# Context scan of a gated DeltaNet: second direction's values and inverses in the other half of the partitions, products in turn with the first's

## The chip, the cores and the metric

The kernel runs on one core of a Trainium2 chip. The core has a matrix engine (TensorE, PE in the profile, with its weight loads as PEld), a vector engine (VectorE, DVE), a scalar engine (ScalarE, ACT), a general one (GpSimd, POOL), and a queue (SyncE, SP) from which most DMA transfers are issued. Each engine takes its instructions in order and waits on semaphores for the others. The metric is the device time of one execution in microseconds (us).

## The reference

One layer of a diffusion backbone over 512 latent tokens and 256 context tokens, model width 1024, everything in float32: a modulated RMS norm, one wide input projection, two mixers side by side (windowed attention; a gated DeltaNet in both directions), a gated sum, an output projection, and a squared-ReLU MLP. Only the latent tokens' result is returned. The part that the change touches is the DeltaNet, with 8 heads of 64 and chunks of 64 tokens:

```python
def gated_delta_chunked(q, k, v, g_log, beta, s0):
    ...
    t_mat = jnp.eye(CHUNK, dtype=jnp.float32) + bc[..., :, None] * dec_strict * kk
    eG = jnp.exp(G)
    w_mat = lax.linalg.triangular_solve(t_mat, (bc * eG)[..., None] * kc, ...)
    u_v = lax.linalg.triangular_solve(t_mat, bc[..., None] * vc, ...)
    intra = dec_incl * jnp.einsum('bhnid,bhnjd->bhnij', qc, kc)
    ...
    def step(S, xs):
        w_c, uv_c, qd_c, intra_c, kt_c, gl_c = xs
        u = uv_c - jnp.einsum('bhck,bhkv->bhcv', w_c, S)
        o = jnp.einsum('bhck,bhkv->bhcv', qd_c, S) + jnp.einsum('bhij,bhjv->bhiv', intra_c, u)
        S = jnp.exp(gl_c)[..., None, None] * S + jnp.einsum('bhck,bhcv->bhkv', kt_c, u)
        return S, o

def bidir_delta(q, k, v, g, beta, s0_f, s0_b):
    o_f, s_f = gated_delta_chunked(q, k, v, g[:, :, 0], beta[:, :, 0], s0_f)
    flip = lambda a: jnp.flip(a, axis=1)
    o_b, s_b = gated_delta_chunked(flip(q), flip(k), flip(v), flip(g[:, :, 1]), flip(beta[:, :, 1]), s0_b)
    return o_f + flip(o_b), s_f, s_b
```

The context (4 chunks) is scanned from a zero state, in both directions, and only its final states are used. The latent tokens (8 chunks) are scanned from those states, and their outputs of the two directions are added.

## The kernel before

Tensors lie with channels on the 128 partitions and tokens along the free axis. Large projections are computed with each operand split in a high and a low part and three matmuls (`mm3`, lines 317 to 319; the gate tiles' L1028 and L1073 are the same three). Weights come 512 KB at a time over the SP queue into four buffers (`wr`); ACT writes the high part (L259) and DVE the low part (L266). The modulation of the later half of the layer is 32 further loads of 512 KB into the same four buffers and a DVE sum for each (`late_mod`, L1092 and L1094), the "late sums".

The instructions are written in one program order, and a planner then orders each engine's queue ahead of time: whatever it reckons to be ready, with the earlier in program order first. `weave` and the numbers in `FILL` set how pieces of work alternate in program order. The *filler* is a generator that yields after every single matmul: 96 of the attention branch's projection (`br_a`, L1073) and 336 of gate tiles (L1028), 432 in all; `run_fill(n)` takes n of them, `run_both(n)` also issues one late sum for every 12, `run_late(n)` issues late sums alone.

The DeltaNet stage runs in these steps. The triangular inverses are computed on DVE (`invert`, L856 and L857) in 32-row halves, then joined by `combine` (L877 to L901: 32x32 products, copies by ACT, zeros by POOL) into `XA[0]` for the context and `XA[1]` for the latent chunks, one tensor for each direction. `to_tokens` (L910, L915) turns keys and values of four chunks to token-major tensors `KTM` and `VTM`: two heads at a time on the two halves of the partitions, a head pair q in columns q*64.

`chain_step(d, step)` is one step of the scan in direction d, a generator in three parts; `steps` runs the two directions' parts one behind the other. Part 1 multiplies the state with the keys (z, L1152; for latent chunks with the queries too) and makes R on DVE (L1156, L1157). Part 2 multiplies R with the inverse (u, L1164) and scales it (L1170). Part 3 multiplies u with the keys (L1185), for latent chunks also with the score matrices `IA` (L1189), and makes the new state (L1199 on ACT, L1201 on DVE). In the second half of the latent scan the two directions' outputs of a chunk are added there and squared and summed (L1211 to L1215). Each product is 64x64 by 64x64, one head in one corner of the array: rows are the half where its operands lie, columns the half where its result goes. In float32 each is two records of the profile.

```python
    weave((steps(range(NCC)), 3 * NCC), (inv, 40), (fill, FILL[0]), (rest(), 9))
```

This line is the context scan: 12 parts of steps, 40 pieces of the latent chunks' inverses, 144 fillers and 9 pieces of `rest` (L657 to L669 and L910). After it come the latent inverses' transposes (L867) and `combine` twice, each with 36 fillers; the score matrices (`half_products`, L777; L1278 to L1289) in two groups g, each with 36 fillers by `run_both`; and the latent scan with 8, 7 and 3 fillers behind the parts and a late sum in each step. Then the normalised output is transposed (L1323) and split (L185), the last three gate tiles run, and the DeltaNet branch's projection begins (`mm3`, weights `wbr[1]`).

Of the kernel before, what the change touches and what calls it, by code (L numbers as in the profile page):

```python
# [12 lines left out]
ALU = mybir.AluOpType  # L13
# [2 lines left out]

NU = 167
NWR, NWS = 4, 2
FILL = 144, 36, 36, (8, 7, 3)
INV = 2, 12, 18, 0  # L20
QTS = 7, 5, 4, 7, 3, 6, 10, 7
CO = 1
# [77 lines left out]
def tile_layer(ctx: ExitStack, tc: tile.TileContext, I: dict, out: bass.AP, dbg=None):  # L100
# [615 lines left out]
    def col(c):  # L716

        return SEQ + c * CH if c < NCC else (c - NCC) * CH
# [150 lines left out]
    def combine(nto, XTf, XRf, XTb, XRb, XAf, XAb, inplace, between=lambda: None):  # L869

        Y, Ys = bank(), alloc(512)
        nt = v3(nto.ap)
        for i in range(16):
            o = slice(i * HC, (i + 1) * HC)
            for a in range(2):
                lo, hi = quad(a, 0), quad(a, 1)
                PE.matmul(Y[hi, o], nt[lo, i], XRf[lo, i], start=True, stop=True)  # L877
                PE.matmul(Y[lo, o], nt[hi, i], XRb[hi, i], start=True, stop=True)
        A.activation(Ys.ap, Y.ap, AF.Copy)
        Y.free()  # L880
        between()
        XO = bank()
        for i in range(16):
            o = slice(i * HC, (i + 1) * HC)
            for a in range(2):
                lo, hi = quad(a, 0), quad(a, 1)
                PE.matmul(XO[lo, o], Ys[hi, o], XTf[hi, i], start=True, stop=True)
                PE.matmul(XO[hi, o], Ys[lo, o], XTb[lo, i], start=True, stop=True)
        Ys.free()
        xo = v3(XO.ap)  # L890
        if not inplace:
            A.activation(XAf[:, :, :HC], XTf, AF.Copy)
            A.activation(XAb[:, :, :HC], XTb, AF.Copy)
        for a in range(2):
            lo, hi = quad(a, 0), quad(a, 1)
            A.activation(XAf[hi, :, HC:], XTf[hi], AF.Copy)
            A.activation(XAb[hi, :, HC:], XTb[hi], AF.Copy)
            A.activation(XAf[lo, :, HC:], xo[lo], AF.Copy)
            A.activation(XAb[hi, :, :HC], xo[hi], AF.Copy)
# [188 lines left out]
    def late_mod(grp):  # L1088

        for j in range(8):  # L1090
            wa = sb.tile([P, KT, P], F32, tag="wr", bufs=NWR, name=nm("wa")).rearrange("p k c -> p (k c)")
            nc.sync.dma_start(out=wa, in_=I["wada2"][grp, j])  # L1092
            t = alloc(1024)
            V.scalar_tensor_tensor(t.ap, wa, 0.5, scr.ap, op0=ALU.mult, op1=ALU.mult, accum_out=modT[:, grp, j:j + 1])  # L1094
# [43 lines left out]
    def chain_step(d, step):  # L1138
# [4 lines left out]
        m4 = slice(c * 4, c * 4 + 4)  # L1143
        z = zb[d]
        r2 = [slice(0, 64), slice(64, 128)]
        vt = VTM[c // 4][:, c % 4 * 256:(c % 4 + 1) * 256]

        if S is not None:
            for q in range(4):
                for x, src in enumerate((kT, qT) if lat else (kT,)):  # L1150
                    for i, r in enumerate(r2):
                        PE.matmul(z[r2[i ^ x], x * 512 + q * HD:x * 512 + (q + 1) * HD], src[q][r, col(c):col(c) + CH],  # L1152
                                  S[r, q * HD:(q + 1) * HD], start=True, stop=True)
# [3 lines left out]
            V.scalar_tensor_tensor(R, vt, -0.5, R, op0=ALU.mult, op1=ALU.add)  # L1157
        else:
            R = vt
        yield  # L1160
        u = z[:, 256:512]
        for q in range(4):
            for r in r2:
                PE.matmul(u[r, q * HD:(q + 1) * HD], XA[lat][d][r, (cl * 4 + q) * CH:(cl * 4 + q + 1) * CH],  # L1164
                          R[r, q * HD:(q + 1) * HD], start=True, stop=True)
        if S is not None:
            Rb.free()
        if not last:
            uk = alloc(256)
            V.tensor_tensor(hv(uk.ap), hv(u), bc(tb[:, d, m4], HD), op=ALU.mult)  # L1170
        if lat:
            us, zqb = alloc(256), alloc(256)
            zq = zqb.ap
# [30 lines left out]
        if lat:  # L1204
            us.free()
            dst = ot_[:, cl * 256:(cl + 1) * 256]
            if step - NCC < NCL // 2:
                V.tensor_tensor(dst, zq, oi[:, :256], op=ALU.add)
                oi.free()
            else:  # L1210
                V.tensor_tensor(zq, zq, oi[:, :256], op=ALU.add)  # L1211
                oi.free()
                V.tensor_tensor(dst, dst, zq, op=ALU.add)
                A.activation(zq, dst, AF.Square)
                V.tensor_reduce(oss[:, cl], hv(zq), axis=AX.X, op=ALU.add)  # L1215
            zqb.free()

    def steps(r):
# [25 lines left out]
    for b in KTM[:1] + VTM[:1] + XA[0]:  # L1244
        b.free()
    scr = alloc(1024, True)
    nc.sync.dma_start(out=scr.ap, in_=I["crow"][0])
# [10 lines left out]
    for g in range(2):  # L1258
        ms = slice(16 * g, 16 * g + 16)
        f, b = xa[0][:, ms], xa[1][:, ms]  # L1260
        run_fill(FILL[1] - CPAUSE)
        combine(NTO[1 + g], f[:, :, :HC], xr3[0][:, ms], b[:, :, :HC], xr3[1][:, ms], f, b, True, lambda: run_fill(CPAUSE))
        NTO[1 + g].free()
    for b in xr:
        b.free()

    IA = [alloc(2048, True), alloc(2048, True)]
    ia = [v64(b.ap) for b in IA]
    for g in range(2):
        ms = slice(16 * g, 16 * g + 16)  # L1270
        es = slice(512 * g, 512 * g + 512)
        run_both(FILL[2] - FPAUSE)
        qq_ = bank(2)
        qD, qO = diag_off(qq_)
        for _ in half_products(qq_, 1 + g, qT):
# [13 lines left out]
            G.memset(ia[1][lo, ms, HC:], 0.0)  # L1289
    for b in ED + [EO]:  # L1290
        b.free()
    dump("kT0", kT[0].ap)
    dump("qT0", qT[0].ap)

    ot_ = alloc(2048, True)
    ot = ot_.ap.rearrange("p (c q v) -> p c q v", c=NCL, q=4)
# [144 lines left out]
    for hf in range(4):  # L1441
        act_ = []
        for f in range(FT):
# [143 lines left out]
```

## Time and profile before

| | |
|---|---|
| time, median of 3 runs | 912.12 us (910.76 to 913.91) |
| the profiled execution | 911.22 us, its span 909.5 us |
| granted TensorE clock | 1.000 |
| instructions | 16844 |
| chain that ended last, by engine | PE 80%, DVE 10%, ACT 5%, issue 2%, DMA 1% |
| HBM read, written | 102.41 MB, 2.10 MB |

A row of a timeline gives start, duration, engine, line, operation, the buffers written and read (numbers left out; `m` is the arena, `banks` PSUM), the shape, how many instructions, and in brackets how long the engine sat idle before it and whose result it waited for. A row of groups or issues gives a count and a mean or median. In a table by stage each engine's busy time stands with its count of instructions in the order PE, PEld, DVE, ACT, POOL, then the granted clock, the DMA engines' share and GB/s. Matmuls overlap, so the duration of one is longer than the distance to the next; a chain of waits gives the time that each piece added.

### The profile page before, as it was taken

What the parts mean: (1) busy time and instruction counts of PE and PEld (TensorE: products, weight loads), DVE (VectorE), ACT (ScalarE), POOL (GpSimd) and SP (SyncE); (2) the same over time, 40 slices, a digit from 0 to 9 for tenths busy, and PEclk for the clock granted to TensorE, in tenths of its full rate; (3) what the DMA queues carried; (4) which work ended last, traced back from release to release, by engine and by line L of the source; (5) the groups of instructions that cost most, each with busy time, mean ns of one, the idle gap of its engine ahead of it and who ended that gap; (6) DMA issues with size and microseconds to landing.
All of it is one profiled execution on the core that took longest, in us unless ns stands there. A gap on an engine that the chain in (4) does not pass through costs nothing.

```text
span 909.5 us, 16844 instructions
## 1 busy us (share of the span) xinstructions
PE 879.4 (97%) x7082; PEld 704.7 (77%) x7082; DVE 585.4 (64%) x999; ACT 454.9 (50%) x819; POOL 25.2 (3%) x40
## 2 busy tenths in 40 slices
PE   8999999999899999999999999999999999999998
PEld 5668777867677787777678789888888888888886
DVE  3578799887778997677867988941654335324511
ACT  6588755476568786465663445630452134113400
POOL 0010001010000002010000000000000000000000
PEclk9999999999999999999999999999999999999999
DMA  8671455533001133633316773640553224322111
GB/s 355 262 230 21 92 117 120 112 71 58 13 13 35 56 110 94 207 98 95 117 37 219 245 245 135 227 144 1 188 157 95 70 73 150 103 69 79 38 47 46
DMA packets 30460, 105.59 MB, mean 116 GB/s; under 512 B 3760, under 2 KB 4400, under 8 KB 29360
## 3 DMA queue, kind: packets, MB, share of 16 engines
q1 hardware_dynamic: 28368, 97.18, 33.1%
q0 software_dynamic: 2016, 7.34, 5.0%
q8 instruction: 55, 0.90, 0.4%
q14 instruction: 21, 0.17, 0.1%
HBM read 102.41 MB, written 2.10 MB: 115 GB/s over the span
## 4 chain that ended last, share of the span: by engine, by line
PE 80%; DVE 10%; ACT 5%; issue 2%; DMA 1%; SPq 0%; DVEq 0%; ACTq 0%
PE banks L319 16%; PE banks L317 16%; PE banks L318 16%; PE banks L1028 9%; PE banks L424 5%; PE banks L1073 2%; PE banks L429 2%; PE banks L586 2%; PE banks L596 1%; PE banks L1164 1%; ACT m L148 1%; PE banks L662 1%; PE banks L1185 1%; PE banks L1152 1%; PE banks L210 1%
## 5 line engine op out<-in xcount | busy, mean ns | idle before, releaser
L317 PE MATMUL banks<-m,m 128*128 128x512 f32 (+1 forms) x600 | 223.6, 377 | 2.6 <-DVE m L643 1.6
L318 PE MATMUL banks<-m,m 128*128 128x512 f32 (+1 forms) x600 | 224.5, 376 | 0.1
L319 PE MATMUL banks<-m,m 128*128 128x512 f32 (+1 forms) x600 | 224.2, 376 | 0.0
L259 ACT ACTIVATE m<-wr 128x1024 fp32r<-128x1024 f32 x68 | 71.8, 1059 | 155.1 <-PE banks L318 74.0
L317 PEld LDWEIGHTS banks<-m,m 128*128 128x128 f32 x600 | 111.8, 188 | 26.0 <-ACT m L323 2.8
L318 PEld LDWEIGHTS banks<-m,m 128*128 128x128 f32 x600 | 112.5, 188 | 21.9 <-DVE m L324 1.5
L319 PEld LDWEIGHTS banks<-m,m 128*128 128x128 f32 x600 | 112.4, 188 | 21.3 <-issue 1.2
L266 DVE TENSOR_TENSOR m<-wr,m 128x1024 fp32r<-128x1024 f32 x68 | 82.8, 1224 | 62.8 <-ACT m L259 31.2
L1028 PE MATMUL banks<-m,wh 128*128 128x512 f32 x320 | 104.5, 405 | 1.5 <-issue 0.8
L1471 DVE SCALAR_TENSOR_TENSOR m<-banks,modT,m 128x512 f32<-128x512 f32 x32 | 24.0, 750 | 105.3 <-PE banks L319 105.3
L259 ACT ACTIVATE wh<-wr 128x1024 fp32r<-128x1024 f32 (+1 forms) x58 | 54.6, 941 | 50.6 <-issue 11.4
L424 PE MATMUL banks<-m,wh 128*128 128x512 f32 (+1 forms) x320 | 75.9, 374 | 1.2 <-DVE m L823 1.2
L1028 PEld LDWEIGHTS banks<-m,wh 128*128 128x128 f32 x320 | 58.0, 188 | 14.2 <-issue 1.0
L1028 PE MATMUL banks<-m,wl 128*128 128x512 f32 x160 | 64.7, 405 | 0.0
L424 PEld LDWEIGHTS banks<-m,wh 128*128 128x128 f32 x320 | 53.0, 189 | 11.5 <-issue 1.9
L266 DVE TENSOR_TENSOR wl<-wr,wh 128x1024 fp32r<-128x1024 f32 (+1 forms) x44 | 45.2, 1028 | 16.6 <-ACT wh L259 16.5
L184 ACT ACTIVATE m<-m 128x512 fp32r<-128x512 f32 (+1 forms) x56 | 34.8, 629 | 38.1 <-DVE m L1454 21.5
L185 DVE TENSOR_TENSOR m<-m,m 128x512 fp32r<-128x512 f32 (+1 forms) x56 | 38.3, 689 | 21.6 <-ACT m L184 21.3
L1094 DVE SCALAR_TENSOR_TENSOR m<-wa,m 128x1024 f32<-128x1024 f32 x32 | 39.0, 1223 | 12.6 <-DMA wa<-in_wada 7.4
L317 PE MATMUL banks<-m,wh 128*128 128x512 f32 (+1 forms) x120 | 42.0, 352 | 0.0
L319 PE MATMUL banks<-m,wl 128*128 128x512 f32 (+1 forms) x120 | 42.0, 351 | 0.0
L318 PE MATMUL banks<-m,wh 128*128 128x512 f32 (+1 forms) x120 | 41.8, 349 | 0.0
(241 smaller groups left out, 1371.8 us busy)
## 6 DMA issues: line engine op xcount, KB each, us to landing
wr<-in_wm SPq DMA_DIRECT2D x64, 512.0 KB, 3.7
wr<-in_win SPq DMA_DIRECT2D x38, 512.0 KB, 3.7
wa<-in_wada SPq DMA_DIRECT2D x32, 512.0 KB, 4.1
m<-in_wada SPq DMA_DIRECT2D x8, 1024.0 KB, 12.3
wl<-in_win POOLq DMA_DIRECT2D x14, 512.0 KB, 5.7
m<-in_xT SPq DMA_DIRECT2D x8, 512.0 KB, 5.6
wr<-in_wbr SPq DMA_DIRECT2D x16, 256.0 KB, 2.6
wr<-in_wout SPq DMA_DIRECT2D x8, 512.0 KB, 4.6
```

The lines of the kernel that those rows point to most:

```text
L184: A.activation(r32(hi), src, AF.Copy)
L185: (eng or V).tensor_tensor(r32(lo), src, hi, op=ALU.subtract)
L259: h = A.activation(r32(hi), raw, AF.Copy)
L266: V.tensor_tensor(r32(lo), raw, hi, op=ALU.subtract)
L317: PE.matmul(acc, w[0][:, k, :], xhi, start=(start and i == 0), stop=False)
L318: PE.matmul(acc, w[0][:, k, :], xlo, start=False, stop=False)
L319: PE.matmul(acc, w[1][:, k, :], xhi, start=False, stop=(stop and i == n - 1))
L424: PE.matmul(a, w[0][:, k, :], x, start=(k == 0 and x is xs[k][0]), stop=False)
L429: PE.matmul(a, w[1][:, k, :], xs[k][0], start=False, stop=(k == KT - 1))
L1028: PE.matmul(acc.ap, w[x][:, k, :], hx[k][y], start=(k == p == 0), stop=(k == KT - 1 and p == 2))
L1094: V.scalar_tensor_tensor(t.ap, wa, 0.5, scr.ap, op0=ALU.mult, op1=ALU.mult, accum_out=modT[:, grp, j:j + 1])
L1471: V.scalar_tensor_tensor(xn_[ct], acc.ap, modT[:, 3, ct:ct + 1], xn_[ct], op0=ALU.mult, op1=ALU.add)
```

## The change

Context scan. Direction 1's inverses are written to the other half of the partitions (`combine`, not in place). Its values are copied to the other half as `vts` by two DMAs on ACT's queue. Direction 1's z then lands in the half where it didn't before, its R lies there, and u comes back to the natural half. Parts 1 and 2 of a context step yield after each head pair, and `steps` calls the directions in turn, so that the program order of the products is direction 0, direction 1, direction 0, and so on. Part 3 is unchanged.

Latent scan. Twelve fillers are taken before the context scan's weave, which has 132 left. The first part of the first latent step is issued between the score matrices' fillers of the second group. A step has 7, 6, 5 fillers. Added outputs are finished one step later, after part 2 (`add_up`).

Late sums. They write over their own load instead of a fresh buffer, and an order without a wait (`behind`) puts each behind the last chain operation that was issued on DVE. `run_both` stands in `combine`'s stage too (6 more there), the latent scan has 4 instead of 8, and the rest are spread anew.

```diff
-FILL = 144, 36, 36, (8, 7, 3)
+FILL = 132, 36, 36, (7, 6, 5)
 ...
         if not inplace:
             A.activation(XAf[:, :, :HC], XTf, AF.Copy)
-            A.activation(XAb[:, :, :HC], XTb, AF.Copy)
         for a in range(2):
             lo, hi = quad(a, 0), quad(a, 1)
+            blo, bhi = (lo, hi) if inplace else (quad(1 - a, 0), quad(1 - a, 1))
             A.activation(XAf[hi, :, HC:], XTf[hi], AF.Copy)
-            A.activation(XAb[hi, :, HC:], XTb[hi], AF.Copy)
+            if not inplace:
+                A.activation(XAb[blo, :, :HC], XTb[lo], AF.Copy)
+            A.activation(XAb[bhi, :, HC:], XTb[hi], AF.Copy)
             A.activation(XAf[lo, :, HC:], xo[lo], AF.Copy)
-            A.activation(XAb[hi, :, :HC], xo[hi], AF.Copy)
+            A.activation(XAb[bhi, :, :HC], xo[hi], AF.Copy)
             G.memset(XAf[hi, :, :HC], 0.0)
-            G.memset(XAb[lo, :, HC:], 0.0)
+            G.memset(XAb[blo, :, HC:], 0.0)
 ...
-            t = alloc(1024)
-            V.scalar_tensor_tensor(t.ap, wa, 0.5, scr.ap, op0=ALU.mult, op1=ALU.mult, accum_out=modT[:, grp, j:j + 1])
-            t.free()
+            op = V.scalar_tensor_tensor(wa, wa, 0.5, scr.ap, op0=ALU.mult, op1=ALU.mult, accum_out=modT[:, grp, j:j + 1])
+            behind(op)
 ...
-        vt = VTM[c // 4][:, c % 4 * 256:(c % 4 + 1) * 256]
-        if S is not None:
-            for q in range(4):
+        sw = 0 if lat else d
+        vt = (vts if sw else VTM[c // 4])[:, c % 4 * 256:(c % 4 + 1) * 256]
+        for q in range(4):
+            if S is not None:
                 for x, src in enumerate((kT, qT) if lat else (kT,)):
                     for i, r in enumerate(r2):
-                        PE.matmul(z[r2[i ^ x], ...
+                        PE.matmul(z[r2[i ^ x ^ sw], ...
+            if not lat:
+                yield
+        if S is not None:
             Rb = alloc(256)
             R = Rb.ap
-            V.tensor_tensor(hv(R), hv(z[:, 0:256]), bc(eG[:, d, m4], HD), op=ALU.mult)
-            V.scalar_tensor_tensor(R, vt, -0.5, R, op0=ALU.mult, op1=ALU.add)
+            V.tensor_tensor(hv(R), hv(z[:, 0:256]), bc((eGs if sw else eG)[:, d, m4], HD), op=ALU.mult)
+            mark[0] = V.scalar_tensor_tensor(R, vt, -0.5, R, op0=ALU.mult, op1=ALU.add)
 ...
         for q in range(4):
-            for r in r2:
-                PE.matmul(u[r, ...], XA[lat][d][r, ...], R[r, ...], start=True, stop=True)
+            for i, r in enumerate(r2):
+                rr = r2[i ^ sw]
+                PE.matmul(u[r, ...], XA[lat][d][rr, ...], R[rr, ...], start=True, stop=True)
+            if not lat:
+                yield
 ...
-                V.tensor_tensor(dst, dst, zq, op=ALU.add)
-                A.activation(zq, dst, AF.Square)
-                V.tensor_reduce(oss[:, cl], hv(zq), axis=AX.X, op=ALU.add)
+                after.append((dst, zqb, cl))
+                return
 ...
+    def behind(op):
+        if mark[0]:
+            tc.add_manual_dep(op.ins, mark[0].ins.name, nosync, reason="behind the chain")
+
+    def add_up():
+        while after:
+            dst, b, cl = after.pop(0)
+            behind(V.tensor_tensor(dst, dst, b.ap, op=ALU.add))
+            A.activation(b.ap, dst, AF.Square)
+            V.tensor_reduce(oss[:, cl], hv(b.ap), axis=AX.X, op=ALU.add)
+            b.free()
 
     def steps(r):
         for step in r:
             both = [chain_step(d, step) for d in range(2)]
-            for _ in range(3):
-                for g in both:
-                    next(g, None)
+            for n, parts in enumerate((1, 1, 1) if step >= NCC else (5, 5, 1)):
+                for _ in range(parts):
+                    for g in both:
+                        next(g, None)
+                if n == 1:
+                    add_up()
                 yield
+        add_up()
 ...
     to_tokens(VTM, vT, 0)
+    vts = alloc(1024, True)
+    for a in range(2):
+        A.dma_start(out=vts[64 * a:64 * a + 64], in_=VTM[0][64 * (1 - a):64 * (1 - a) + 64])
     to_tokens(KTM, kT, 0)
+    run_fill(12)
 ...
-        run_fill(FILL[1] - CPAUSE)
-        combine(NTO[1 + g], ..., True, lambda: run_fill(CPAUSE))
+        run_both(FILL[1] - CPAUSE)
+        combine(NTO[1 + g], ..., True, lambda: run_both(CPAUSE))
 ...
+    scan = steps(range(NCC, NC_))
     for g in range(2):
-        run_both(FILL[2] - FPAUSE)
+        if g:
+            run_both(FPAUSE)
+            next(scan)
+        run_both(FILL[2] - (1 + g) * FPAUSE)
 ...
-    for n, _ in enumerate(steps(range(NCC, NC_))):
+    for n, _ in enumerate(scan, 1):
         run_fill(FILL[3][n % 3])
-        if n % 3 == 2:
+        if n % 3 == 1 and n < 3 * NCL // 2:
             run_late(1)
 ...
     for _ in gate_tiles(gates[12 + NGD:]):
         pass
+    run_late(2)
 ...
-        run_late(ct % 2)
+        run_late(ct in (2, 5))
 ...
-            if hf == 0:
-                next(late)
+            if hf == 0 and f >= NHALF:
+                for _ in range(1 + (f > NHALF + 1)):
+                    next(late)
```

More of the change, by code (lines that the diff above doesn't have):

```diff
@@ L1162, in chain_step @@
         for q in range(4):
-            for r in r2:
-                PE.matmul(u[r, q * HD:(q + 1) * HD], XA[lat][d][r, (cl * 4 + q) * CH:(cl * 4 + q + 1) * CH],
-                          R[r, q * HD:(q + 1) * HD], start=True, stop=True)
+            for i, r in enumerate(r2):
+                rr = r2[i ^ sw]
+                PE.matmul(u[r, q * HD:(q + 1) * HD], XA[lat][d][rr, (cl * 4 + q) * CH:(cl * 4 + q + 1) * CH],
+                          R[rr, q * HD:(q + 1) * HD], start=True, stop=True)
+            if not lat:
+                yield
         if S is not None:
@@ L1169, in chain_step @@
             uk = alloc(256)
-            V.tensor_tensor(hv(uk.ap), hv(u), bc(tb[:, d, m4], HD), op=ALU.mult)
+            mark[0] = V.tensor_tensor(hv(uk.ap), hv(u), bc(tb[:, d, m4], HD), op=ALU.mult)
         if lat:
@@ L1212, in chain_step @@
                 oi.free()
-                V.tensor_tensor(dst, dst, zq, op=ALU.add)
-                A.activation(zq, dst, AF.Square)
-                V.tensor_reduce(oss[:, cl], hv(zq), axis=AX.X, op=ALU.add)
+                after.append((dst, zqb, cl))
+                return
             zqb.free()
+    after, mark = [], [None]
+    def behind(op):
[8 more added lines that the diff above has]
+            b.free()
     def steps(r):
@@ L1243, in tile_layer @@
         pass
-    for b in KTM[:1] + VTM[:1] + XA[0]:
+    for b in KTM[:1] + VTM[:1] + [vts] + XA[0]:
         b.free()
@@ L1260, in tile_layer @@
         f, b = xa[0][:, ms], xa[1][:, ms]
-        run_fill(FILL[1] - CPAUSE)
-        combine(NTO[1 + g], f[:, :, :HC], xr3[0][:, ms], b[:, :, :HC], xr3[1][:, ms], f, b, True, lambda: run_fill(CPAUSE))
+        run_both(FILL[1] - CPAUSE)
+        combine(NTO[1 + g], f[:, :, :HC], xr3[0][:, ms], b[:, :, :HC], xr3[1][:, ms], f, b, True, lambda: run_both(CPAUSE))
         NTO[1 + g].free()
```

5 lines of the change are left out of this document (2 added, 3 removed).

## The prediction

> **What bounds the kernel now.** I read the page's busy shares first, then a table by stage, then the TensorE timeline of the two scans.
>
> ```profile
> PE 879.4 (97%) x7082; PEld 704.7 (77%) x7082; DVE 585.4 (64%) x999; ACT 454.9 (50%) x819; POOL 25.2 (3%) x40
> ```
> TensorE (PE) is busy nearly always. The table by stage (columns: stretch, length, then busy time of each engine) says where it is not:
> ```profile
> 190.00:290.00 100.00, 93.38 (x760) 71.55 (x759) 75.13 (x131) 69.05 (x124) 3.81 (x6) 1.00 0.13 30
> 290.00:346.80 56.80, 55.38 (x545) 42.28 (x543) 52.96 (x108) 47.98 (x110) 0.34 (x1) 1.00 0.27 80
> 346.80:394.30 47.50, 46.83 (x925) 37.10 (x924) 30.04 (x39) 24.74 (x42) 7.39 (x14) 1.00 0.48 149
> 394.30:474.70 80.40, 74.80 (x1442) 57.96 (x1433) 59.22 (x130) 50.25 (x159) 1.48 (x2) 1.00 0.30 89
> 474.70:560.00 85.30, 84.95 (x452) 72.02 (x451) 70.28 (x116) 36.65 (x58) 0.00 (x0) 1.00 0.66 213
> ```
> 290 to 346.8 is the context scan, to 394.3 the combining of the latent inverses, to 474.7 the latent scan. PE idles 1.4, 0.7 and 5.6 us there, 0.35 us after. So two things count: PE work taken out, and those 7.7 us.
>
> The chain of waits shows what PE work a scan product is (start, us, what):
> ```profile
> 308.91 1.08 PE banks L1152 x32
> 309.98 2.98 PE banks L1073 x12
> 312.97 1.08 PE banks L1164 x32
> 413.41 1.09 PE banks L1152 x64
> ```
> In the context scan a set of products of both directions is 32 records (16 products, two records each) in 1.08 us, 33.7 ns apiece, between 12 filler matmuls; its places in the array alternate between two corners. In the latent scan the same line sends 64 records in 1.09 us, 17.0 ns apiece: there keys and queries go to different corners and all four are used in turn. That row is the price of the change's main idea, measured on the same tile shape.
>
> **The change, part by part.**
>
> *Products in turn.* Direction 1 now multiplies in the two unused corners, and its products alternate with direction 0's, for z (L1152, steps 1 to 3) and u (L1164, steps 0 to 3). Seven sets of 32 records; L1185 stays as it is. A set in full rotation costs 32 x 17.0 ns = 0.545 us and saves 0.535. But TensorE takes its queue in order and the planner puts ready work first, so a set only alternates if both directions' operands are there when it is reached. For z they come early. For u the last operand is direction 1's R (L1157):
> ```profile
> 312.40 0.42 DVE L1157 SCALAR_TENSOR_TENSOR m<-m,m 128x256 f32<-128x256 f32 x1
> 326.08 0.42 DVE L1157 SCALAR_TENSOR_TENSOR m<-m,m 128x256 f32<-128x256 f32 x1
> 339.82 0.42 DVE L1157 SCALAR_TENSOR_TENSOR m<-m,m 128x256 f32<-128x256 f32 x1
> ```
> It ends at 312.82, 326.50, 340.24, and PE takes the sets up at 312.97 and, in the rows below, 327.75 and 341.67: 0.15, 1.25 and 1.43 us to spare. The new filler share (132 over 12 parts: 11 matmuls, not 12) takes one matmul, 2.98/12 = 0.25 us, off each. So z: 3 x 0.535 = 1.6 us. u: two steps of three, 1.07; step 0 none, since its halves already ran apart (next fence). Term: **-2.7 us**, between 0 (nothing alternates) and 7 x 0.535 = -3.75.
> ```profile
> 327.75 1.08 PE banks L1164 x32
> 341.67 1.08 PE banks L1164 x32
> ```
>
> [...]
>
> *Twelve fillers ahead of the scan.* PE timeline:
> ```profile
> 291.91 1.30 PE L910 MATMUL banks<-c_ident,m 128*128 128x128 f32 x8 [0.20 <-DVE m L649]
> 294.10 1.04 PE L1164 MATMUL banks<-m,m 64*64 64x64 f32 x16 [0.89 <-ACT m L915]
> 299.47 0.68 PE L1164 MATMUL banks<-m,m 64*64 64x64 f32 x16
> 303.92 1.15 PE L1185 MATMUL banks<-m,m 64*64 64x64 f32 x32
> ```
> PE waits 0.89 us for the first copies to tokens. Twelve fillers (2.98 us) cover that: **-0.9** (0 to -1.09, the two waits).
>
> *The swapped values (vts).* Two ACT-issued copies, 64 partitions each, between SBUF halves; no such copy is in the trace. Nearest rows:
> ```profile
> wr<-in_win SPq DMA_DIRECT2D x38, 512.0 KB, 3.7
> wr<-in_wbr SPq DMA_DIRECT2D x16, 256.0 KB, 2.6
> 293.57 6.31 ACT L915 ACTIVATE m<-banks 64x256 f32<-64x256 f32 x16
> 345.99 0.33 SPq L250 DMA_DIRECT2D wr<-in_win  x1
> 361.48 0.59 ACT L899 ACTIVATE m<-banks 32x512 f32<-32x512 f32 x1
> ```
> Half of the L915 copies are done at 296.7; two issues (0.33 each) and 2.6 to 3.7 us make 300.0 to 301.1, against 299.47 when direction 1's first products ran. If the planner puts too little filler there, PE waits up to 1.6 us; it can also be nothing. I take **+0.3**, near the lower end, since fillers are ready there. Behind the issues on ACT stand the key copies; they end at 299.9, would end 0.7 later, and L1185 took them at 303.9: covered. The swapped XA costs one more ACT copy of 32 partitions (0.59, as L899) in the attention stage, 190 to 290, where ACT is busy 69.05 of 100 and PE 93.38: mostly covered, **+0.2** for issues and copy (0 to 0.66 + 0.59 = +1.25).
>
> *Latent scan.* PE's waits there:
> ```profile
> 379.47 0.73 PE L1028 MATMUL banks<-m,wh 128*128 128x512 f32 x2 [0.67 <-ACT m L148]
> 400.48 1.15 PE L1164 MATMUL banks<-m,m 64*64 64x64 f32 x32 [1.74 <-DVE m L1157]
> 405.31 0.69 PE L1152 MATMUL banks<-m,m 64*64 64x64 f32 x32 [0.40 <-DVE m L1201]
> 435.87 0.68 PE L1164 MATMUL banks<-m,m 64*64 64x64 f32 x16 [1.09 <-DVE m L1157]
> 444.25 1.15 PE L1164 MATMUL banks<-m,m 64*64 64x64 f32 x32 [0.74 <-DVE m L1157]
> 462.85 0.68 PE L1164 MATMUL banks<-m,m 64*64 64x64 f32 x16 [0.35 <-DVE m L1157]
> ```
> and what VectorE (DVE), and ACT ahead of the first of them, did meanwhile:
> ```profile
> 375.82 2.03 ACT L1199 ACTIVATE m<-m,egl 128x64 f32<-128x64 f32 x8 [1.33 <-DVE m L1094]
> 397.39 1.83 DVE L1285 COPY m<-m 32x512 f32<-32x512 f32 x4
> 403.70 1.22 DVE L1094 SCALAR_TENSOR_TENSOR m<-wa,m 128x1024 f32<-128x1024 f32 x1
> 441.31 0.41 DVE L1213 TENSOR_TENSOR m<-m,m 128x256 f32<-128x256 f32 x1
> 441.64 1.22 DVE L1094 SCALAR_TENSOR_TENSOR m<-wa,m 128x1024 f32<-128x1024 f32 x1
> 461.23 1.22 DVE L1094 SCALAR_TENSOR_TENSOR m<-wa,m 128x1024 f32<-128x1024 f32 x1
> ```
> - The 1.74: the first R stands on DVE behind the scores' copies (L1285). Issued 24 fillers earlier it is out of the way, but u's scaling (L1170) and the output products now stand behind those copies: **-1.2** (0 to -1.74).
> - 0.40 + 0.74 + 0.35 = 1.49: a late sum (L1094, 1.22 us) or a last sum (L1213 and the reduction after it) ahead of a chain step. The change orders them behind: **-1.2** (0 to -1.49).
> - 0.67: ACT held by a buffer that L1094 wrote; in place there is none: **-0.4** (0 to -0.67).
> - The 1.09 has another cause (DVE held by a gate tile and a weight split); 0.
> - New: 7, 6, 5 fillers in place of 8, 7, 3. One filler is 0.25 us less cover after z and after u, eight steps each, where the 0.35 to 1.74 us waits above show little slack: **+0.8** (0 to 16 x 0.25 = +4; the two extra after the third part, 0.5 a step, give half back, so +2).
>
> *Late sums elsewhere.* Twelve of them now fall between 346.8 and 394.3, where DVE idles 17.5 us, in place of six; fewer later. After 474.7 PE idles 0.35 us of 85.3, so nothing is to be won there; the filler and weights hide them. 0, between -0.35 and one sum, +1.22.
>
> *Does the end follow?* The branch after the scan needs the last split:
> ```profile
> 479.90 0.69 DVE L185 TENSOR_TENSOR m<-m,m 128x512 fp32r<-128x512 f32 x1
> 474.71 11.38 PE banks L1028 x49
> ```
> It is ready at 480.6, PE is in gate tiles until 486.1. PE can gain 5.5 us before it would wait, even if DVE's chain (52.96 of 56.80 us busy in the context stage) got no shorter. With 7 fillers left over for the tail, the cover holds.
>
> Sum: -2.7 - 0.9 + 0.3 + 0.2 - 1.2 - 1.2 - 0.4 + 0.8 = **-5.1 us**. The profiled execution took 911.22 us (span 909.5 and 1.7 around it): 906.1. The median of the runs, 912.12, lies 0.9 above it: **907.0**.
>
> **Rivals.**
> 1. *Nothing alternates.* If R of direction 1 comes after PE has begun direction 0's, PE runs 16 and 16 as at 294.10 and 299.47. Sum -2.4: **909.7**. For it: 0.15 us of slack in step 1. Against: over 1 us in the others, more for z.
> 2. *The waits come back elsewhere.* PE's order is fixed when the program is planned; the chip's times differ, and the latent terms (-2.8) turn up at other places. Sum -2.3: **909.8**. For it: six waits of different cause in 85 us.
> 3. *Slower: late loads hold VectorE.* A late sum whose 512 KB have not landed stops DVE, and the next gate weights' low half (L266) behind it:
> ```profile
> 363.30 1.23 DVE L1094 SCALAR_TENSOR_TENSOR m<-wa,m 128x1024 f32<-128x1024 f32 x1 [3.75 <-DMA wa<-in_wada]
> 379.04 1.23 DVE L1094 SCALAR_TENSOR_TENSOR m<-wa,m 128x1024 f32<-128x1024 f32 x1 [3.25 <-DMA wa<-in_wada]
> ```
> Six more of them wait up to 6 x 3.75 = 22.5 us; DVE's 17.5 idle less their own 6 x 1.22 = 7.3 leaves 10.2 of cover. It decides from 10.2 + 5.1 = 15.3 us of waiting. At 18.9, midway to 22.5, the kernel is 3.6 us slower: **915.7**. Against: PE did not stop for L266 at these two; its 0.67 near the second was on ACT.
> 4. *A floor on starts* for alternating products, somewhere between the measured 17.0 and 33.7 ns apiece: at the middle, 25.4, a set saves 0.27, five save 1.35, and the sum is -3.75: **908.4**. [...] The 64-record row speaks against it.
>
> **Chances and range.** Forecast 0.62, rival 1 0.12, rival 2 0.11, rival 3 0.11, rival 4 0.02, else 0.02. A measurement of this kernel tells 0.3% (2.7 us) from no change, so faster is below 909.4: forecast, rival 4 and a third of rivals 1 and 2, 0.72; same 0.16; slower 0.12. The likeliest's own range: all gains in full, -3.75 - 1.09 - 1.74 - 1.49 - 0.67 = -8.7, is 903.4, up to 909.4. The range reaches from 903.0 to 912.0, over rivals 1 and 2; rival 3 is left out.
>
> **What would show it.** Right: L1152 and L1164 in the context scan as mixed sets of 32 records in about 0.55 us; L1185 still 1.08; no 0.89 us wait at the scan's start; in the latent scan no wait of L1164 on L1157 with L1094 ahead of it; PE idle between 290 and 475 about 5 us, not 7.7; br_dn's first matmul 5 us earlier and the tail unchanged. Wrong: sets still 1.08, a wait of L1164 for the vts copy over 1.6 us, or PE waiting on L266 behind an L1094 that waits for its load.

## The result: slightly slower, 915.16 us, and the profile after

The changed kernel took 915.16 us (median of 11 runs, 914.04 to 917.99), the kernel before beside it 912.88 (11 runs, 910.76 to 916.13). The ratio is 1.0028, 95% interval 1.0017 to 1.0039. I had forecast 907.0 with a range of 903.0 to 912.0: wrong in sign, and out by 8.2 us. The profiled execution took 914.04 us (span 912.3), 2.8 more than the one before.

The busy shares hardly differ from before:

```profile
PE 880.7 (97%) x7082; PEld 705.7 (77%) x7082; DVE 587.4 (64%) x999; ACT 455.3 (50%) x820; POOL 25.1 (3%) x40
```

The table by stage does (columns: stretch, length, busy time of PE, PEld, DVE, ACT, POOL, then the granted clock, DMA share, GB/s). The kernels drift by some us against the fixed cuts, so a wait near a cut can fall on either side:

```profile
190.00:290.00 100.00, 93.03 (x752) 71.13 (x751) 73.26 (x128) 68.05 (x122) 3.80 (x6) 0.98 0.12 28
290.00:346.80 56.80, 54.70 (x525) 41.09 (x523) 53.82 (x108) 47.82 (x110) 0.00 (x0) 1.00 0.31 93
346.80:394.30 47.50, 44.05 (x872) 35.03 (x873) 35.11 (x51) 25.07 (x43) 7.60 (x14) 0.96 0.56 180
394.30:474.70 80.40, 79.31 (x1514) 61.62 (x1513) 62.32 (x131) 51.19 (x159) 1.48 (x2) 1.00 0.32 97
474.70:560.00 85.30, 82.78 (x430) 69.91 (x429) 65.61 (x104) 36.33 (x55) 0.00 (x0) 1.00 0.61 201
```

TensorE's idle time (length less busy) fell from 5.6 to 1.1 us in the latent scan, more than forecast, and rose from 1.4 to 2.1 in the context scan, 0.7 to 3.4 in the combining and 0.35 to 2.5 from 474.7 to 560. Two stretches have a clock below 1.00; before had none.

The main idea works. The chain of waits shows sets of 32 products in 0.62 us (1.08 before), L1154 being z and L1170 u, while L1193, which was not changed, still takes 1.08:

```profile
313.12 0.62 PE banks L1154 x32
...
316.49 0.62 PE banks L1170 x32
...
320.73 1.08 PE banks L1193 x32
```

What went against it are these waits of TensorE, all new but the first, which is what is left of the 0.89 us before (timeline; in brackets the idle time and who ended it):

```profile
296.62 1.05 PE L1170 MATMUL banks<-m,m 64*64 64x64 f32 x16 [0.64 <-ACT m L917]
335.31 1.09 PE L912 MATMUL banks<-c_ident,m 128*128 128x128 f32 x8 [0.67 <-ACT m L1077]
348.27 1.15 PE L1193 MATMUL banks<-m,m 64*64 64x64 f32 x32 [1.91 <-DVE m L1178]
370.70 0.24 PE L878 MATMUL banks<-m,m 32*32 32x32 f32 x2 [1.47 <-issue]
554.34 0.70 PE L1431 MATMUL banks<-m,ones 128*128 128x256 f32 x2 [1.09 <-DVE m L1408]
557.53 0.62 PE L317 MATMUL banks<-m,m 128*128 128x256 f32 x3 [1.20 <-ACT m L323]
567.72 0.50 PE L317 MATMUL banks<-m,m 128*128 128x256 f32 x2 [0.48 <-ACT m L323]
```

The last three stand at the MLP's norm, where the kernel before waited 0.3 us. (Two waits on ScalarE in the attention stage also grew: the one for the copies of the inverses, L901, from 0.60 to 0.85 us, and one for L148 from 0.77 to 0.90.) VectorE shows why: late sums (L1095), the first held by its load, stand ahead of the residual's square sums (L1408) that the norm needs:

```profile
552.72 1.23 DVE L1095 SCALAR_TENSOR_TENSOR wa<-wa,m 128x1024 f32<-128x1024 f32 x1 [1.34 <-DMA wa<-in_wada]
553.87 0.08 DVE L1095 DVE_READ_ACCUMULATOR wa<-wa,m 128x1 f32 x1
553.87 0.42 DVE L1408 TENSOR_TENSOR m<-m,m 128x256 f32<-128x256 f32 x1
...
554.68 1.22 DVE L1095 SCALAR_TENSOR_TENSOR wa<-wa,m 128x1024 f32<-128x1024 f32 x1
555.83 0.08 DVE L1095 DVE_READ_ACCUMULATOR wa<-wa,m 128x1 f32 x1
555.83 0.42 DVE L1408 TENSOR_TENSOR m<-m,m 128x256 f32<-128x256 f32 x1
```

The clock: at 242 us TensorE waits 2.09 us in both kernels for the same VectorE instruction. Before, the products behind that wait run at full speed (granted clock 1.00 from 243.7 to 248.6 us); this is the kernel before:

```profile
243.70 0.96 PE L586 MATMUL banks<-m,m 128*128 128x512 f32 x3 [2.09 <-DVE m L185]
...
244.68 0.60 PE L596 MATMUL banks<-c_ident,m 128*128 128x128 f32 x4
```

and this the changed one, the same instructions with the clock granted at 0.50 from 245.18 to 248.60 us:

```profile
244.91 1.44 PE L586 MATMUL banks<-m,m 128*128 128x512 f32 x3 [2.08 <-DVE m L185]
...
246.47 1.05 PE L596 MATMUL banks<-c_ident,m 128*128 128x128 f32 x4
```

Two such stretches of 3.41 us at half clock, here and behind the 1.47 us stop at 370 (from 371.48 us), cost up to 3.41 x 0.5 = 1.7 us each, by my estimate. The profiled execution of the kernel before, at 1.000, was not typical of it: averaged over the runs the granted clock was 0.9945 after, and 0.9972 for the 35 runs of the kernel before that stand beside e1 to e4, one of them at 1.000. That difference is worth 0.0027 x 913 = 2.5 us, as much as the medians differ by. So at like clock the two kernels are about level: the new waits ate what the change won, and half clock made it slower.

### The profile page after: what moved, and what is told of

Same layout as the page of the kernel before. It is cut to its first block, busy times and chain, and to the rows that moved or that the text cites. A ratio compares the mean times of both kernels' runs of the same rounds, so it can differ in the third digit from the quotient of the medians.

```text
span 912.3 us, 16853 instructions
## 1 busy us (share of the span) xinstructions
PE 880.7 (97%) x7082; PEld 705.7 (77%) x7082; DVE 587.4 (64%) x999; ACT 455.3 (50%) x820; POOL 25.1 (3%) x40
## 4 chain that ended last, share of the span: by engine, by line
PE 79%; DVE 11%; ACT 6%; issue 3%; DMA 2%; SPq 0%; DVEq 0%; ACTq 0%
PE banks L317 15%; PE banks L318 15%; PE banks L319 15%; PE banks L1030 10%; PE banks L424 5%; PE banks L429 2%; PE banks L1075 2%; PE banks L586 2%; PE banks L596 1%; PE banks L1154 1%; DVE wl L266 1%; PE banks L1170 1%; PE banks L662 1%; ACT wh L259 1%; PE banks L1193 1%
## 5 line engine op out<-in xcount | busy, mean ns | idle before, releaser
L266 DVE TENSOR_TENSOR m<-wr,m 128x1024 fp32r<-128x1024 f32 x68 | 83.1, 1224 | 72.7 <-PE banks L318 43.3
L266 DVE TENSOR_TENSOR wl<-wr,wh 128x1024 fp32r<-128x1024 f32 (+1 forms) x44 | 45.2, 1028 | 8.5 <-ACT wh L259 8.2
L1095 DVE SCALAR_TENSOR_TENSOR wa<-wa,m 128x1024 f32<-128x1024 f32 x32 | 38.8, 1222 | 13.5 <-DMA wa<-in_wada 13.5
```

Source lines behind the costliest of these rows:

```text
L266: V.tensor_tensor(r32(lo), raw, hi, op=ALU.subtract)
L1095: op = V.scalar_tensor_tensor(wa, wa, 0.5, scr.ap, op0=ALU.mult, op1=ALU.mult, accum_out=modT[:, grp, j:j + 1])
```

## Experiments

Every ratio is to the kernel before, run beside it on the same chip (its medians were 912.8 to 913.7); differences in us between two kernels are of medians where nothing else is said. "Clock" is the granted clock averaged over a kernel's runs; 0.0019 is one stretch, 1.7 us. "At full clock" is an estimate from these runs: each run's time less 913 us x (1 - its clock), the median of that, less the same for the kernel before (for "after", less each of the four groups of runs of the kernel before that stand beside the experiments). Three theories stood at the start. A: the products in turn pay, and the re-placed late sums take it back. B: VectorE ends the context scan anyway, so the turn only makes TensorE wait. C: half clock after short idle times makes the difference.

| kernel | median us | ratio, 95% interval | clock | at full clock, us |
|---|---|---|---|---|
| after | 915.16 | 1.0028 (1.0017 to 1.0039) | 0.9945 | -0.1 to -0.5 |
| e1_rot | 917.35 | 1.0040 (1.0023 to 1.0056) | 0.9956 | +2.6 |
| e2_norot | 915.95 | 1.0024 (1.0008 to 1.0041) | 0.9949 | +0.4 |
| e3_lateold | 916.61 | 1.0035 (1.0013 to 1.0057) | 0.9947 | +1.4 |
| e4_mlpold | 913.40 | 0.9997 (0.9977 to 1.0016) | 0.9958 | -1.3 |
| e5_behind | 911.86 | 0.9981 (0.9961 to 1.0001) | 0.9966 | -2.6 |
| e6_gapfill | 913.91 | 1.0016 (1.0001 to 1.0030) | 0.9969 | +0.3 |
| e7_rotx | 912.98 | 1.0003 (0.9992 to 1.0015) | 0.9975 | -0.1 |
| e8_lateoldx | 911.66 | 0.9990 (0.9974 to 1.0006) | 0.9977 | -1.4 |
| e9_fill144 | 912.18 | 0.9989 (0.9974 to 1.0003) | 0.9968 | -1.9 |
| e10_fillgap | 911.43 | 0.9982 (0.9968 to 0.9996) | 0.9978 | -1.8 |
| e11_norot | 915.06 | 1.0026 (1.0008 to 1.0044) | 0.9954 | -0.1 |
| e12_quiet | 910.27 | 0.9964 (0.9950 to 0.9978) | 0.9973 | -4.0 |
| e13_spread | 916.36 | 1.0034 (1.0020 to 1.0048) | 0.9972 | +2.9 |
| e14_beforegap | 911.48 | 0.9986 (0.9975 to 0.9997) | 0.9991 | -0.4 |
| e15_quietgap | 909.88 | 0.9959 (0.9946 to 0.9972) | 0.9972 | -3.7 |

### Parts undone or done alone: e1 to e4

*e1_rot*: the kernel before, with the diff's hunks for XA, `sw`, `vts` and the parts (5, 5, 1) only.

> The kernel before with the products in turn alone (swapped values and inverses, z and u sharing their sets; fillers, late sums and latent scan as before). In the profile of the changed kernel six sets of 32 products took 0.69 us busy instead of 1.15, which is worth 6 x 0.5 = about 3 us of TensorE. Theory A (the turn pays, the re-placed late sums take it back): 909 to 910.5 us, ratio 0.996 to 0.998, with no 1.5 us wait of L1185 on VectorE. Theory B (VectorE's chain ends the context scan anyway, so that the turn only makes TensorE wait): 912 to 913.5, ratio 0.999 to 1.001, and a wait of 1 to 2 us of the last L1185 on VectorE. Theory C (stretches of half clock, 1.7 us each, make the difference): the mean granted clock says it: at 0.998 or above the time follows theory A, with each further 0.002 of clock 1.8 us more.

*e2_norot*: the changed kernel without these hunks.

> The changed kernel with the products in turn undone (corners, values and order of products as before; fillers, latent scan and late sums as changed). Theory A (the turn is worth about 3 us, the late sums cost more): 917 to 919 us, ratio 1.005 to 1.007. Theory B (the turn is swallowed by VectorE): 914.5 to 916, ratio 1.002 to 1.004, as the changed kernel. Theory C (half-clock stretches): clock 0.992 to 0.996 whatever the edit, and the time moves by 1.7 us with each stretch more or less.

*e3_lateold*: the changed kernel with

```diff
-            op = V.scalar_tensor_tensor(wa, wa, 0.5, scr.ap, ..., accum_out=modT[:, grp, j:j + 1])
-            behind(op)
+            t = alloc(1024)
+            V.scalar_tensor_tensor(t.ap, wa, 0.5, scr.ap, ..., accum_out=modT[:, grp, j:j + 1])
+            t.free()
```

and `run_both`, `run_late` and `next(late)` in the combining, the scan, the column tiles and the MLP as before.

> The changed kernel with the late sums as before in place, buffer and order (a buffer of their own, one each third step of the scan, none beside the combining, one a column tile afterwards, one a feature tile in the first half of the MLP); turn, fillers and latent scan as changed. Theory A (the re-placed late sums cost the 1.47 us stop in the combining, the 2.3 us of waits at the MLP's norm and a half-clock stretch after the first): 908.5 to 911, ratio 0.996 to 0.999. Theory B (the turn does not pay and the late sums cost nothing): 914 to 916. Theory C (half-clock stretches come with any short wait): clock still 0.992 to 0.996 and 913 to 915.

*e4_mlpold*: the changed kernel with the MLP's placement alone undone.

```diff
-            if hf == 0 and f >= NHALF:
-                for _ in range(1 + (f > NHALF + 1)):
-                    next(late)
+            if hf == 0:
+                next(late)
```

> The changed kernel with one thing undone: the last eight late sums stand again one at each feature tile of the MLP's first half. If the waits at the MLP's norm (1.09, 1.20 and 0.48 us, none of them in the kernel before) come from late sums that VectorE does ahead of the residual: they go, 912 to 913 us, ratio 0.999 to 1.001. If they come from the sums before, which this leaves (two ahead of the branches' output, one at column tiles 2 and 5): they stay, 914.5 to 916.

Measured: 917.35, 915.95, 916.61, 913.40. Neither e1_rot nor e3_lateold fits any theory as I had put it: both medians lie above the changed kernel's. The profile of e1_rot shows a cause that belongs to neither part:

```profile
511.62 1.75 SPq L1373 DMA_DIRECT2D m<-in_xT  x4
...
518.26 0.75 DVE L1383 SCALAR_TENSOR_TENSOR m<-banks,gt1h,m 128x512 f32<-128x512 f32 x1 [0.88 <-DMA m<-in_xT]
...
524.36 0.50 PE L317 MATMUL banks<-m,wh 128*128 128x512 f32 x1 [3.65 <-ACT wh L259]
```

The four loads of the residual's input (2 MB) go out at 511.6, ahead of the output weights; in the kernel before they go out at 482 and 488. The buffers that the turn adds shift the ring of free memory, xT's buffer comes to lie where the late sums' scratch buffers were, and its loads wait for them. e3_lateold has the same (508.2 us, a wait of 3.5). So both said nothing of what they were made for, and were repeated as e7 and e8. e4_mlpold is 1.8 us below the changed kernel, 1.2 of them by its higher clock; waits of 1.0 and 0.8 us at the norm remain in its profile, so the MLP's placement is only part of that cause. e2_norot fell into theory B's range, within its interval of the changed kernel; but its profile has an extra stop of 2.28 us in the combining, so that its time says little of the turn. Its context scan says more; it stands in the table in the part on the prediction.

### The order before the norm, the idle wait, and the two repeats: e5 to e8

*e5_behind*: the changed kernel, and in `norm()` the mark behind which late sums must stay, set to the last instruction of its last `modulate`:

```diff
             t.free()
+        mark[0] = lastmod[0]
```

> The changed kernel with one order added: the last eight late sums may not stand on VectorE ahead of the last product of the MLP norm's second half. If the late sums pulled ahead of the residual make the waits at the norm (1.09, 1.20 and 0.48 us in the changed kernel): these go, 912 to 913.5 us, ratio 0.999 to 1.001. If TensorE simply comes there too early for VectorE's other work: they stay or come back as waits of like length, 914.5 to 916.

*e6_gapfill*: the changed kernel, in `values()` behind the first product of unit (2, 0):

```diff
+    for _ in range(6):
+        dm = PE.matmul(db.ap, r32(VS[:, 0:128]), r32(KH[0][:, 0:512]), start=True, stop=True)
+        tc.add_manual_dep(dm.ins, mm.ins.name, nosync, reason="in the gap")
```

> The changed kernel with six idle products of 128x512 (about 1.4 us, results unused) put into TensorE's 2.09 us wait in the attention stage at 242 us; nothing else moves. [...] Rival (half clock has nothing to do with that wait): half clock there again, clock 0.994 to 0.995, 915 to 916, ratio 1.002 to 1.004. If the products hold TensorE up: 915 to 917 at a higher clock.

*e7_rotx* and *e8_lateoldx*: e1_rot and e3_lateold, with the free memory above unit 130 closed while `X1` is allocated.

> The products in turn alone, as in e1_rot, but with the buffer of the residual's input (xT) kept out of the place of the late sums' scratch buffers, so that its four loads do not wait for them. Theory (in e1_rot the loads of xT came late, at 511 us, ahead of the output weights, and made a wait of 3.65 us and a half-clock stretch): xT issued before 495 us, no wait over 1 us before L317 between 505 and 530, 5 us less than e1_rot, 911 to 913, ratio 0.997 to 1.000; the turn itself then shows at the end of the context scan, 1.5 to 2.5 us ahead of e1_rot's waits. Rival (weights come too late there whatever xT does): 916 to 918.

> The changed kernel with the late sums as before (as e3_lateold), and the buffer of xT placed as in e7_rotx. Theory (e3_lateold was 4.5 us ahead of the kernel before at the end of the latent scan and lost 3.5 us plus a half-clock stretch of 1.7 to xT's late loads): 909.5 to 912, ratio 0.995 to 0.999. Rival (the gain of the two scans is lost at the MLP's entry to VectorE or the weights in any case): 914 to 917.

Measured: e5 911.86. All TensorE waits of e5_behind from 474.7 to 575 us, in one line:

```profile
PE banks L317 <- ACT m L325: 0.3, 1, 0.3
```

The waits of 1.09, 1.20 and 0.48 are gone, and with them 3.3 us (2.1 to 2.5 at full clock): the order on VectorE was the cause, not TensorE's being early (it began the DeltaNet branch's projection 4.4 us earlier than in the changed kernel and still did not wait). e5's profiled execution, which happened to have no half clock (1.000), took 907.86 us.

e6: clock from 0.9945 to 0.9969, 1.1 us less by the ratios, the side of theory C; e14 tests theory C by itself. e7: xT's loads at 483 and 489, 4.4 us less than e1_rot, no wait on weights: the memory placement was e1's cause. The turn alone ends level with before (1.0003): in its profile TensorE idles 6.6 us in the latent scan (5.6 before) and 2.1 at the norm (0.3 before). There, with the late sums where they always were, two of them stand ahead of the norm's products on VectorE, where the kernel before has one. So the re-placing is not needed for waits at the norm: the shift of the planned order that the turn makes brings them too. e8: 911.66, 4.9 less than e3_lateold; its waits at the norm, behind a weight split, add up to 1.5.

### The fillers, the turn, the combining: e9 to e12

*e9_fill144*: e5_behind with

```diff
-FILL = 132, 36, 36, (7, 6, 5)
+FILL = 144, 36, 36, (7, 6, 5)
...
-    run_fill(12)
```

> e5_behind with the twelve fillers put back from ahead of the context scan into it (144 in the scan, none ahead). Theory (the twelve at the start saved 0.25 us of a 0.89 us wait and uncovered VectorE's end of the scan, 1.92 and 0.64 us): the wait of the last L1193 falls from 1.92 to 0.3 us as in e7_rotx, 1 to 1.7 us less than e5_behind, 910 to 911 us, ratio 0.996 to 0.998; fewer half-clock stretches would make it 909.5. Rival (VectorE ends the context scan wherever the fillers stand): the 1.92 stays, 911.5 to 912.5, ratio 0.998 to 0.9995.

*e10_fillgap*: e9 with e6's idle products. *e11_norot*: e9 without the turn (e2's hunks).

> e9_fill144 with the six idle products in the 2.09 us wait of the attention stage, as in e6_gapfill. [...] Rival: as e9_fill144, clock 0.996 to 0.997.

> e9_fill144 with the products in turn undone. Theory A (the turn saves TensorE 6 x 0.5 = 3 us in the context scan, and e7_rotx gained 2.0 there): 1.5 to 3 us more than e9_fill144, 911.5 to 913, ratio 0.998 to 1.000. Theory B (VectorE's chain takes the gain): within 0.7 us of e9_fill144.

*e12_quiet*: e9 with

```diff
-        run_both(FILL[1] - CPAUSE)
+        run_fill(FILL[1] - CPAUSE)
...
-        if n % 3 == 1 and n < 3 * NCL // 2:
+        if n % 3 == 1:
```

and `run_fill(CPAUSE)` for `run_both(CPAUSE)` between the two product loops.

> e9_fill144 with no late sums beside the combining of the latent inverses (only fillers there; late sums at each step's second part in the whole latent scan instead, the rest at the column tiles). The stop of about 1 to 2.3 us in TensorE among the 32x32 products at 367 to 371 us stood in every kernel with late sums there (after 1.47, e2_norot 2.28, e4_mlpold 1.03, e5_behind 0.96, e6_gapfill 1.54) and was 0.5 or less without them (before, e1_rot, e3_lateold, e7_rotx, e8_lateoldx). [...] Rival (chance): a stop of about 1 us there again.

Measured: e9 912.18. The wait at the scan's end fell as the theory said, and the one at 335 with it, but the total did not, since a new wait took its place. From e9's timeline (VectorE's, then TensorE's; L1097 is the late sum here, L1032 a gate tile, L266 the low half of its weights):

```profile
363.94 1.23 DVE L1097 SCALAR_TENSOR_TENSOR wa<-wa,m 128x1024 f32<-128x1024 f32 x1 [1.37 <-DMA wa<-in_wada]
...
365.70 1.22 DVE L266 TENSOR_TENSOR wl<-wr,wh 128x1024 fp32r<-128x1024 f32 x1
...
346.44 1.15 PE L1195 MATMUL banks<-m,m 64*64 64x64 f32 x32 [0.29 <-DVE m L1180]
...
366.97 0.50 PE L1032 MATMUL banks<-m,wl 128*128 128x512 f32 x1 [1.94 <-DVE wl L266]
```

Late sums whose loads have not landed hold VectorE, and TensorE waits for the weights' low half behind them: rival 3 of the prediction, as it was described there, at 1.94 us. e12_quiet takes the late sums out of the combining: that wait is gone, and 910.27 (0.9964) is below both kernels. The stop among the 32x32 products did not go with the late sums, though:

```profile
367.24 0.24 PE L880 MATMUL banks<-m,m 32*32 32x32 f32 x2 [1.36 <-issue]
```

And e12 pays elsewhere: the last eight sums, all behind the norm since e5, stand among the weights and activations ahead of the MLP's second product, where the kernel before had no wait. All waits of TensorE in e12's profile from 575 to 640 us (the mean clock of that execution is 0.998, as one half-clock stretch makes it):

```profile
PE banks L317 <- ACT m L184: 1.9, 1, 1.9
PE banks L318 <- DVE m L185: 0.4, 1, 0.4
```

e11: without the turn 915.06 (1.0026), 2.9 us above e9, theory A. Of these, 1.3 are its lower clock (0.9954 against 0.9968), which leaves 1.6 (1.8 by the column); its profile has a 2.69 us stop in the combining. e10: 0.75 us below e9 at a higher clock (0.9978), in theory C's direction; the intervals overlap.

### The stop and the clock by themselves: e13 to e15

*e13_spread*: e12 with `run_fill(1)` after every second `i` of both product loops of `combine` (fourteen fillers fewer ahead of it).

> e12_quiet with one filler matmul after each eighth of the 32x32 products of the latent combining (fourteen for each group of heads, taken from the fillers ahead of it), so that 64 products take about 2.7 us in place of 1.1 and TensorE uses up its instructions more slowly. [...] Rival (the stop belongs to the products or their banks): a stop of about 1 us remains; if going from 32x32 to 128x128 and back costs, 911 or more.

*e14_beforegap*: the kernel before with e6's idle products; *e15_quietgap*: e12 with them.

> The kernel before with the six idle products in the 2.09 us wait of the attention stage. [...] Rival: clock and time as before, ratio 1.000.

> e12_quiet with the six idle products in the same wait. Theory: mean clock from 0.9973 to 0.9985 or above, 0.7 to 1.2 us less than e12_quiet, 909 to 909.6 us, ratio 0.995 to 0.996. Rival: as e12_quiet.

Measured: e13 916.36. The stop went (the longest wait left from 350 to 395 us is 0.37), yet the kernel is 6.1 us slower. One group of 64 products with seven fillers took 4.9 us, where 1.08 and 7 x 0.25 make 2.8. In the table by stretch TensorE has no idle time there, so I put the rest down to the changes between 32x32 and 128x128 products, by estimate (4.9 - 2.8) / 7 = 0.3 us for each way there and back:

```profile
353.60:359.00 5.40, 5.40 (x137) 3.33 (x137) 5.37 (x6) 4.37 (x7) 0.72 (x2) 1.00 0.01 3
```

What holds TensorE in the stop is not shown. In the profile after, a 16 KB packet of the queue q8 starts at 368.40 us, and the stop ends 2.30 us later, at 370.70; in e2_norot such a packet stands between 369 and 370, and the stop ends at 371.52. No row shows that the one waits for the other. What the late sums have to do with the stop is open too: e12 has none there and stops 1.36 us.

e14: the only change is the filled wait, in a kernel that is otherwise the one before. Clock 0.9974 to 0.9991, seven of its twelve runs at 1.000, and 1.3 us less (0.9986). The idle time in the profile:

```profile
241.86 1.53 PE L592 MATMUL banks<-m,m 128*128 128x512 f32 x6
244.12 0.96 PE L586 MATMUL banks<-m,m 128*128 128x512 f32 x3 [0.72 <-DVE m L185]
```

The products behind it start no earlier than before (244.12, in an execution that runs 0.4 us late by then); only the clock changed. So in the kernel before this idle time did bring half clock in some of its runs, 0.0017 of clock on the mean. e15: 909.88, the lowest median here, 0.4 below e12 at about the same mean clock (0.9972): the rival's side. What makes the half clock that is left in its profiled execution (0.997) is not shown.

## Why the prediction was wrong, step by step

- **Products in turn, -2.7.** Right in mechanism, too large in size: all three z and u of steps 1 to 3 alternate, step 0's u runs apart. A set takes 0.62 us, not 0.545, so six sets are 6 x 0.46 = 2.8 us shorter. What arrives is less. From the start of the first u to the start of the last set of u with the keys (L1164 and L1185 in the kernel before), the profiles give:

  | us | 144 fillers in the scan | 132, and 12 ahead |
  |---|---|---|
  | without the turn | 51.6 (before, e11_norot) | 52.8 (e2_norot) |
  | with the turn | 49.6 (e7_rotx, e9_fill144) | 51.7 (after) |

  The turn is worth 2.0 us there with 144 fillers and 1.1 with 132, where VectorE ends the scan: theory B in part. The wait ahead of the first u falls by 0.25 with it. The rest of the 2.8 I cannot place, but for the 0.29 us wait at e9's end of the scan. Rival 1 is out, and so is rival 4 at its 25.4 ns: 0.62 / 32 = 19.4 ns apiece.
- **Twelve fillers ahead, -0.9.** Failed, and the term was about +2: the table has +1.2 without the turn and +2.1 with it, so in the changed kernel they took back all that the turn had won in the scan. They did not cover the wait at the start either. It is 0.88 us in e2_norot, which has them, and 0.63 in e7_rotx, which has not: it fell with the turn. On the chip the twelve stand behind the first u, 23 matmuls in place of 12 between the halves of step 0's u, and are missing at the scan's end, where VectorE is late: 1.91 and 0.67 us of waits. I took the place in the program for the place on the chip, and named no work that hid the end, though I had VectorE at 52.96 of 56.80 us. e9 puts them back and has 0.29 and nothing.
- **vts +0.3, copies +0.2.** No wait for the vts copy shows. The copies cost 0.3 to 0.4: TensorE's waits in the attention stage are 6.2 to 6.3 us in three profiles without the turn (before, e2, e11) and 6.6 in four with it (after, e5, e7, e9).
- **Latent scan, -2.0 in all.** Right in sign, too small: idle 5.6 to 1.1 us. The 1.74 is gone (a wait of 0.62 at 406.53 is new), and the 0.8 for fewer fillers does not show. But 1.94 us of the gain are luck: the wait of 1.09, which I had put at 0, and a stop of 0.85 at 415.34 us, which I had not listed, are gone too, and why is not shown. The 0.67 became 0.51.
- **Late sums elsewhere, 0.** The step that failed worst. I wrote that nothing could be won after 474.7 because TensorE idles 0.35 us there, bounded the loss by one sum (+1.22), and took the filler and weights as the cover. VectorE's order ahead of the norm was that cover: it cost 2.5 us of new waits, and undoing them was worth 3.3 us (e5; 2.1 to 2.5 at full clock). "Does the end follow" had the same fault: I looked at the next wait of the chain, the branch's projection, and not at the norm behind it. That projection began 0.4 us later than before (486.3 against 485.9), where I had said 5 earlier.
- **Rival 3** had the right mechanism and happened at smaller prices, beside the norm (552.72) and in e9 (1.94). I had asked of it 15 us of waiting before it decided; it takes far less, since VectorE's idle time is not where the loads are waited for. That its 915.7 lies near the measured 915.16 is luck: the combining, where it was to happen, shows no such wait in the changed kernel.
- **No term at all** for the half clock (3.4 us in the profile after, 0 before; 2.5 by the mean clocks of the runs) and for the stop of 1.47.

The sum again, profile to profile: turn -2.8, copies +0.4, start -0.25, scan's end +1.91 + 0.67, latent scan -4.5, stop +1.47, norm +2.5, half clock +3.4, together +2.8; measured +2.8. That it meets so closely is chance: the turn's full 2.8 does not arrive, and other waits moved by some tenths. With the norm mended and no half clock, one execution of e5 took 907.86, against 911.22 for the one before at the same clock of 1.000: 3.4 less, where the forecast said 5.1.

## What to carry over

Price a re-placed piece of work, where the planner puts it and not where the program has it, at every consumer that the engine serves behind it, by that engine's order and its transfers, not by the idle time of the engine that is the bound: a stage without idle time can lose, and it is the cover that goes. Count what a wait costs after it as well: here a wait of 2.08 us was followed by 3.41 us at half clock, worth 1.7 us. And when one part of a change is tested alone, look first whether buffers and transfers lie where they did, or the test answers another question.

## What the runs showed of the hardware

- In the profile after, TensorE's clock is granted at 0.50 in two stretches of 3.413 us ahead of the last 1.5 us of its span, from 245.18 and from 371.48 us. The first begins 0.27 us after a wait of 2.08 us had ended, the second 0.78 us after the stop of 1.47 us. No half clock followed the wait of 1.91 us that ended at 348.27 in the same profile, nor the one of 2.09 us that ended at 243.70 in the kernel before; how much idle time brings it is not shown. Filling that wait raised the mean clock of the kernel before from 0.9974 to 0.9991 (e14). The runs' spread follows the clock: over the 35 runs of the kernel before beside e1 to e4, 0.001 of clock goes with 0.93 us, correlation -0.93.
- 64x64 products over all four corners go at 19.4 ns apiece in sets of 32 (0.62 us a set in the profile after); a change from 32x32 to 128x128 products and back cost 0.3 us in e13, by the estimate above (4.9 us in place of 2.8, seven changes).
- TensorE stopped in a burst of 32x32 products for 1.47 us in the changed kernel, 2.28 in e2_norot and 1.36 in e12_quiet; in e13_spread, with fillers among the products, it had no idle time in the three stretches of them (22.9 us). The cause is not shown.
